# The output stage's loads of merged rows, post-norm vector, kept tiles and x rows spread over products and pinned to their traced place

## The chip, the cores and the metric

One core of one Trainium2 chip. The core has a matrix engine (TensorE, PE), a vector engine (VectorE, DVE), a scalar engine (ScalarE, ACT), GpSimd (POOL) and a sync engine (SyncE, SP); in this kernel nearly every DMA is issued from SP's queue. The metric is device microseconds of the whole program; the time before is the median of three runs.

## The reference

One layer of a bidirectional encoder with 1024 rows and model width 2048, in float32. What the output stage computes is the last two lines of `hybrid_layer`:

```python
h = rmsnorm(x, pre_g) * (1.0 + scale[:, None]) + shift[:, None]
proj = h @ w_in
...
merged = g_a * (y_a @ w_br_attn) + g_p * (y_p @ w_br_pool)
o = merged @ w_out                                   # (1024, 2048) @ (2048, 2048)
return x + gate[:, None] * rmsnorm(o, post_g)
```

`rmsnorm` takes the mean square over all 2048 columns of a row of `o`, so a row of the output can be finished only when all of its columns are there.

## The kernel before

**Products.** Every large matrix product is made with float32 operands that are split into a high and a low part (`split`, L95 on ACT for the high part, L96 on DVE for the low part), and three matmuls: high by high, low by high, high by low. Two-by-two blocks of a product are formed with seven block products instead of eight, so sums of blocks (S1 to S4 of the weights, T1 to T4 of the moving rows) take the place of one product. S1 to S4 of `w_out` were written to DRAM (`ws_d`) earlier in the program.

**The output stage** is four calls of `out_pair(half, i, ...)`: half 0 and 1 are the first and second 512 rows, i is the first or second block of 512 columns in each half of the columns. In words below they are pairs 00, 01, 10 and 11. Each pair runs seven products in this order: A11 by B11 (bank X), S3 by T3 (V), S2 by T2 (Z), A12 by B21 (X), A22 by T4 (V), S1 by T1 (Z), S4 by B22 (Z). They are numbered n = 0 to 6 where the code says `n`. One product takes four weight loads of 512 KB, `wr`, from `ws_d` (L1174) or `w_out` (L1177), into a ring of four buffers; each load is split into two pairs `whi`, `wlo` (rings of four); 48 matmuls follow (L1183 to L1185), 24 for each of two banks, twelve for each load. A load can go when the splits of the load four before it, which had its buffer, have been made. The four loads of the next pair's A11 are issued in the middle of S4 (`first_raws`).

**Work between the products.** After each quarter of a product (jp = 0 to 3) a hook runs: `between_00` to `between_11`, by pair. In `between_00` it splits the merged rows for the next product (`put_op`, tiles `m` into `mh` on ACT and `ml` on DVE) and loads merged rows of the second half into the `m` tiles (`fetch_next`, `fetch_merged`, L1168; 16 loads of 256 KB in eight calls of two). There are eight such tiles, each filled by two loads. They hold the first half's merged rows, and a tile is free once its last split was made: the four of `kh` = 0 in the quarters of A22, the four of `kh` = 1 in those of S1. In pair 01 the sums and splits for the second half are made; in pairs 10 and 11 the first half's rows are finished (`first_rows`: a kept tile of `o` from `o_d`, L1342, and the row of x, L1209, into a ring of eight row tiles `mo`; `finish_block`, L1204, and its store, L1205), and x rows for the last rows are loaded (`xr`).

**Results.** Behind a product its banks are taken out by ACT or DVE (`p7`, `u2`, `c11`, `u4`), squared with a row sum on ACT (`square`, L1193), and multiplied with the post-norm vector `pg` (`result`, L1273; `pg` is loaded by `fetch_gain`, L1229, in two loads). Pair 00 stores its results to `o_d` (L1277); the other pairs keep them.

**Order.** A scheduler sets the order of each engine's instructions, by its own estimates, except for instructions given to `keep`: such an instruction keeps its place behind the one traced before it on its engine. All loads and stores of the stage (`load`, `store`) are issued by SP in the order of its program. An issue that waits for its buffer, or for its data, holds all that are behind it.

Of the kernel before, what the change touches and what calls it, by code (L numbers as in the profile page):

```python
# [12 lines left out]
F32 = mybir.dt.float32  # L13
# [7 lines left out]
P = 128  # L21
# [21 lines left out]
def encoder_layer(ctx: ExitStack, tc: tile.TileContext, x, c, table, w_ada, b_ada, pre_g,  # L43
# [16 lines left out]
    x = x[0]  # L60
# [4 lines left out]
    def pool(name, bufs=1, **kw):  # L65
        return tc.tile_pool(name=name, bufs=bufs, reuse_waits="tile", **kw)
# [9 lines left out]
    def uid(s):  # L76
        cnt[0] += 1
        return f"{s}_{cnt[0]}"
# [4 lines left out]
    def slot(name, dt=F32R, shape=(P, 512)):  # L83
        return big.tile(list(shape), dt, tag="big", name=uid(name))
# [5 lines left out]
    def keep(ins):  # L90

        tc.keep_in_program_order(ins)
# [14 lines left out]
    load = nc.sync.dma_start  # L107
# [15 lines left out]
    JP = KT // 4  # L123
# [9 lines left out]
    o_d = dram.tile([S // 2, D], F32, name="o_d")  # L133
    ws_d = {n: dram.tile([D // 2, D // 2], F32, name=f"ws_d{n}") for n in ("S1", "S2", "S3", "S4")}
    m_d = dram.tile([D, S], F32, name="m_d")
    pg_d = dram.tile([1, D], F32, name="pg_d")
# [215 lines left out]
    for r0, src in ((0, c[0]), (16, b_ada[0, 0:D]), (32, b_ada[0, D:2 * D]),  # L352
                    (48, pre_g[0]), (64, b_merge[0]), (96, pool_scale[0])):
        n = src.shape[0] // P
# [421 lines left out]
    held = {}  # L776
# [38 lines left out]
    with pool("attn") as ap:  # L815
# [27 lines left out]
        qraw, q, bt, g, pr, pv, opened = {}, {}, {}, {}, {}, {}, []  # L843
# [240 lines left out]
    for b, w in enumerate((w_ba, w_bp)):  # L1084
# [4 lines left out]
        else:  # L1089
# [4 lines left out]
            mr = ctx.enter_context(pool("mraw", side="right"))  # L1094

            def merged_tiles():

                return [[mr.tile([P, 2, 512], F32, tag="m", name=uid("m"), bufs=2 * JP) for _ in range(JP)]
                        for _ in range(2)]
# [65 lines left out]
    def fetch_merged(m, kh, jp):  # L1165
        for n in range(2):
            k = 2 * (2 * jp + n) + kh
            load(m[kh][jp][:, n], m_d[k * P:(k + 1) * P, 512:1024])  # L1168

    def weights(name, i, jp):  # L1170

        raw = wp.tile([P, 2, 512], F32, tag="raw", name=uid("wr"), bufs=4)
        if name in ws_d:
            load(raw, ws_rows(name)[:, 2 * jp:2 * jp + 2, i * 512:(i + 1) * 512])  # L1174
        else:
            n0 = (name[1] == "2") * (D // 2) + i * 512
            load(raw, wo_rows(int(name[2]) - 1)[:, 2 * jp:2 * jp + 2, n0:n0 + 512])  # L1177
        return raw

    def out_mm(pb, op, name, j, t, w, first, last):  # L1180
        ts_ = slice(t * P, (t + 1) * P)
        hi, lo = (o_[:, j % 2, ts_] for o_ in op[name][j // 2])
        nc.tensor.matmul(pb, hi, w[0], start=first, stop=False, skip_group_check=True)  # L1183
        nc.tensor.matmul(pb, lo, w[0], start=False, stop=False, skip_group_check=True)  # L1184
        nc.tensor.matmul(pb, hi, w[1], start=False, stop=last, skip_group_check=True)  # L1185

    xrow, held = {}, {}
# [18 lines left out]

    def fetch_x_block(T, n, tile_of):
        xrow[T, n] = tile_of("xr")
        load(xrow[T, n], x[T * P:(T + 1) * P, n * 512:(n + 1) * 512])  # L1209

    def row_tiles():
        m = mr.tile([P, 2, 512], F32, tag="m", name=uid("mo"), bufs=2 * JP)
# [4 lines left out]
    def out_pair(half, i, op, between, after=None):  # L1217
# [5 lines left out]
        g = {}  # L1223

        def fetch_gain():
            for nh in range(2):
                g[nh] = ev.tile([P, 512], F32, tag="ev", name=uid("pg"))
                n0 = nh * (D // 2) + i * 512
                load(g[nh], pg_d[0:1, n0:n0 + 512].to_broadcast([P, 512]))  # L1229

        def split_weights(wname, ring=True, pin=()):
            for jp in range(JP):
                raw = first_raws.pop(0) if wname == "A11" and first_raws else weights(wname, i, jp)
                for jj in range(2):
                    hi, lo = (wp.tile([P, 512], F32R, tag=t, name=uid(t), bufs=4) if ring else slot(t)
                              for t in ("whi", "wlo"))
                    split(hi, lo, raw[:, jj], 2 * jp + jj in pin)
                    yield hi, lo


        def product(wname, mov, pbs, fresh=False):

            ws = split_weights(wname)
            n, nj = next(count), 2 * JP
            for j in range(nj - 2):
                w = next(ws)
                for t in range(2):
                    out_mm(pbs[t], op, mov, j, t, w, fresh and j == 0, False)
                if j % 2:
                    between(n, j // 2)  # L1250
            w = list(ws)
            if n == 6:
                first_raws.extend(weights("A11", 1 - i, jp) for jp in range(JP))
            for t in range(2):
                for j in (nj - 2, nj - 1):
                    out_mm(pbs[t], op, mov, j, t, w[j - nj + 2], False, j == nj - 1)
            between(n, JP - 1)
# [5 lines left out]
        def copies(ts, pbs):  # L1263
            for t in range(2):
                nc.scalar.activation(ts[t], pbs[t], AF.Copy)
            return ts
# [12 lines left out]
        def kept(tag):  # L1279

            return list(row_tiles()) if half == 1 and i == 0 else tiles(tag)
# [1 line left out]
        bx, bz, bv = ([bank(tag, b) for tag in tags] for b, tags in  # L1283
                      (("X", ("mm", "mm")), ("Z", SEEDED), ("V", ("sc", "sc"))))
        product("A11", "B11", bx, True)
        fetch_gain()
        for t in range(2):
            nc.scalar.activation(bz[t], bx[t], AF.Copy)
        product("S3", "T3", bv, True)
        p7 = copies(kept("p7"), bv)  # L1290
        product("S2", "T2", bz)
        u2 = copies(kept("u2"), bz)
# [31 lines left out]
            for n in (0, 2, 3, 1):  # L1324
                finish_block(6 + t, n, scale)

    nextm, nextt2 = [], {}
    scales = {}
    side = deque()

# [2 lines left out]
    def first_rows(T, n):  # L1333

        def place(name):
            ring.rotate(-1)
            return ring[-1]

        def fetch():
            if (T, n) not in held:  # L1340
                held[T, n] = place("fo")
                load(held[T, n], o_d[T * P:(T + 1) * P, n * 512:(n + 1) * 512])  # L1342
            fetch_x_block(T, n, place)

        def put_out():
            if T not in scales:
                scales[T] = row_scale(T)
            finish_block(T, n, scales[T])

        return fetch, put_out  # L1350
# [6 lines left out]
    later = deque((kh, jp) for kh in range(2) for jp in range(JP))  # L1357

    def fetch_next():
        if later:  # L1360
            fetch_merged(nextm, *later.popleft())

    def between_00(n, jp):
        if n < 6:
            put_op(n + 1, jp, ops[0], mt, mt2)
        if n == 4 and jp == JP - 1:
            nextm.extend(merged_tiles())
        if n >= 5 and jp:
            fetch_next()

    def between_01(n, jp):

        if n == 0 and jp:
            fetch_next()
        if n == 1:
            merged_sums(nextm, nextt2, jp)
        for k in ((), (), (0,), (1, 2), (3,), (4,), (5,))[n]:
            put_op(k, jp, ops[1], nextm, nextt2)
# [17 lines left out]
    def between_11(n, jp):  # L1396
        if jp % 2 and n < 3:
            steps(1)
        if jp == JP - 1 and n in (2, 4):
            for T in (4, 5) if n == 2 else (6, 7):  # L1400
                for b in range(4):
                    fetch_x_block(T, b, lambda name: slot(name, F32))

    def third_block():
        assert not side
# [47 lines left out]
```

## Time and profile before

| | us |
|---|---|
| median of three runs | 2126.83 |
| lowest and highest of them | 2126.15, 2128.21 |
| the profiled execution's own time | 2129.34 |
| its span | 2127.5 |
| output stage: first matmul of A11 of pair 00 | 1804.94 |
| first matmul of A11 of pairs 01, 10, 11 | 1886.33, 1964.17, 2040.47 |
| last matmul ends | 2119.05 |

The granted clock of PE is 0.999 in the profiled execution, so it takes no part in what follows. PE, DVE, ACT and POOL are the engines; SP's queue of issues is shown as SPq. A row of a timeline has the start of an instruction from the span's start in us, its duration, engine, source line, operation, output and inputs by the program's names (numbers left out), and in brackets the idle time before it on its engine, with the instruction that ended it. "A <- B" in a list of waits says that A's engine was idle until B, with the total in us, how often, and the longest. For a DMA issue the duration is the time until the queue went on, with all waits for its condition in it; "to landing" is from the issue to the arrival of the data. Product starts are times of the first matmul of a product on PE.

### The profile page before, as it was taken

The numbers are of one execution on the slowest core, as the hardware profiler recorded it, in microseconds if no ns is written. First come the engines' busy times: TensorE is split into PE (matmuls) and PEld (weight loads), VectorE is DVE, ScalarE is ACT, GpSimd is POOL, SyncE is SP. The second block draws the span as 40 slices with busy tenths as digits, with TensorE's granted clock in tenths as the row PEclk, the third lists the DMA queues.
The fourth block names the chain that finished last, engine by engine and source line by source line (L and its number), as shares of the span: only waits on it lengthen the run. The fifth ranks groups of instructions, "written<-read, shape, count | busy, mean of one in ns | idle before, by whom it ended". The sixth has DMA issues, their size and how long they took to land.

```text
span 2127.5 us, 28921 instructions
## 1 busy us (share of the span) xinstructions
PE 2091.2 (98%) x9567; PEld 1713.4 (81%) x9567; DVE 1536.2 (72%) x2754; ACT 1106.6 (52%) x2102; POOL 7.4 (0%) x66
## 2 busy tenths in 40 slices
PE   6999999999999999999999999999999999999998
PEld 3588888887888888888888888888788788878876
DVE  5786667777547776677777678856857977879667
ACT  5654444444474544665656444333645644768655
POOL 0000000000000000000000000000000000000000
PEclk9999999999999999999999999999999999999999
DMA  9886566899676355544645576765745654686896
GB/s 327 272 269 217 186 206 224 301 309 315 223 232 207 122 177 200 169 162 159 201 145 164 158 243 221 224 210 187 252 158 174 218 184 161 225 294 220 303 303 244
DMA packets 303255, 466.10 MB, mean 219 GB/s; under 512 B 23883, under 2 KB 144867, under 8 KB 303105
## 3 DMA queue, kind: packets, MB, share of 16 engines
q1 hardware_dynamic: 301648, 462.02, 66.0%
q0 software_dynamic: 1120, 2.19, 0.3%
q8 instruction: 75, 1.23, 0.2%
q14 instruction: 76, 0.61, 0.1%
q10 hardware_dynamic: 336, 0.06, 0.0%
HBM read 340.41 MB, written 125.85 MB: 219 GB/s over the span
## 4 chain that ended last, share of the span: by engine, by line
PE 88%; DVE 5%; DMA 4%; issue 1%; ACT 1%; SPq 1%; ACTq 0%; DVEq 0%
PE Z L235 30%; PE X L235 20%; PE V L235 20%; PE Z L1183 2%; PE Z L1184 2%; PE Z L1185 2%; PE V L1185 1%; PE V L1183 1%; PE V L1184 1%; DMA raw<-in_w_merge_dram 1%; PE GEMV L455 1%; PE X L1185 1%; DVE wlo L96 1%; PE X L1184 1%; PE X L1183 1%; PE PT L905 1%
## 5 line engine op out<-in xcount | busy, mean ns | idle before, releaser
L95 ACT ACTIVATE whi<-raw 128x512 fp32r<-128x512 f32 (+1 forms) x528 | 321.3, 610 | 509.7 <-PE Z L235 254.3
L96 DVE TENSOR_TENSOR wlo<-raw,whi 128x512 fp32r<-128x512 f32 (+1 forms) x528 | 347.4, 662 | 183.7 <-PE Z L235 132.8
L96 DVE TENSOR_TENSOR wlo<-wr,whi 128x512 fp32r<-128x512 f32 x224 | 151.1, 689 | 60.9 <-ACT whi L95 58.4
L95 ACT ACTIVATE whi<-wr 128x512 fp32r<-128x512 f32 x224 | 138.7, 629 | 93.5 <-DVE wlo L96 37.2
L102 DVE TENSOR_TENSOR raw<-raw,raw 128x512 f32<-128x512 f32 x80 | 55.2, 690 | 107.0 <-DMA raw<-in_w_merge_dram 79.1
L235 PE MATMUL V<-T3h,whi 128*128 128x512 f32 x336 | 92.1, 393 | 0.7 <-DVE u L102 0.5
L235 PE MATMUL Z<-T2h,whi 128*128 128x512 f32 x336 | 91.6, 392 | 0.8 <-ACT whi L95 0.7
L235 PE MATMUL X<-B11h,whi 128*128 128x512 f32 x336 | 92.1, 392 | 0.0
L235 PE MATMUL Z<-B22h,whi 128*128 128x512 f32 x336 | 91.6, 392 | 0.5 <-ACT u L290 0.5
L235 PE MATMUL V<-T4l,whi 128*128 128x512 f32 x336 | 91.2, 390 | 0.7 <-DVE T4l L96 0.6
L235 PE MATMUL V<-T4h,whi 128*128 128x512 f32 x336 | 91.4, 391 | 0.2 <-ACT T4h L95 0.2
L235 PE MATMUL Z<-T1h,whi 128*128 128x512 f32 x336 | 91.6, 390 | 0.0
L235 PE MATMUL X<-B11l,whi 128*128 128x512 f32 x336 | 91.0, 390 | 0.0
L235 PE MATMUL X<-B21h,whi 128*128 128x512 f32 x336 | 91.0, 391 | 0.0
L235 PE MATMUL Z<-T2h,wlo 128*128 128x512 f32 x336 | 90.8, 390 | 0.1
L235 PE MATMUL X<-B21l,whi 128*128 128x512 f32 x336 | 90.8, 390 | 0.0
L235 PE MATMUL Z<-B22l,whi 128*128 128x512 f32 x336 | 90.7, 390 | 0.0
L235 PE MATMUL Z<-T1l,whi 128*128 128x512 f32 x336 | 90.7, 389 | 0.0
L235 PE MATMUL X<-B11h,wlo 128*128 128x512 f32 x336 | 90.7, 390 | 0.0
L235 PE MATMUL Z<-B22h,wlo 128*128 128x512 f32 x336 | 90.6, 390 | 0.1
L235 PE MATMUL V<-T3l,whi 128*128 128x512 f32 x336 | 90.6, 389 | 0.0
L235 PE MATMUL Z<-T1h,wlo 128*128 128x512 f32 x336 | 90.6, 389 | 0.0
(308 smaller groups left out, 4771.7 us busy)
## 6 DMA issues: line engine op xcount, KB each, us to landing
part<-part_d SPq DMA_DIRECT2D x136, 256.0 KB, 4.9
ada<-in_w_ada_dram SPq DMA_DIRECT2D x128, 256.0 KB, 5.4
raw<-in_w_in_dram SPq DMA_DIRECT2D x64, 512.0 KB, 4.0
raw<-in_w_merge_dram SPq DMA_DIRECT2D x64, 512.0 KB, 5.8
wr<-ws_dS SPq DMA_DIRECT2D x64, 512.0 KB, 5.6
wr<-in_w_out_dram SPq DMA_DIRECT2D x48, 512.0 KB, 5.1
proj_d<-part SPq DMA_DIRECT2D x68, 256.0 KB, 2.3
sw<-in_w_out_dram SPq DMA_DIRECT2D x64, 256.0 KB, 5.5
```

The lines of the kernel that those rows point to most:

```text
L95: ins = (nc.scalar.activation(hi, src, AF.Copy), nc.vector.tensor_tensor(lo, src, f32(hi), ALU.subtract))
L96: nc.vector.tensor_tensor(lo, src, f32(hi), ALU.subtract))
L102: return (eng or nc.vector).tensor_tensor(o, a, b, ALU.add)
L235: nc.tensor.matmul(ps, w_[:, i], op[mov][j][m_], start=fresh and i == 0 and n == 0, stop=i == nj - 1 and n == 2, skip_group_check=True)
L455: ins = nc.tensor.matmul(pv[g:g + 32, :], scz[:, kc, :], tile_of(kc), start=kc < 4, stop=kc >= 12, tile_position=(0, g))
L905: nc.tensor.transpose(pt[:, i * P:(i + 1) * P], p[:, i * P:(i + 1) * P], ident)
L1183: nc.tensor.matmul(pb, hi, w[0], start=first, stop=False, skip_group_check=True)
L1184: nc.tensor.matmul(pb, lo, w[0], start=False, stop=False, skip_group_check=True)
L1185: nc.tensor.matmul(pb, hi, w[1], start=False, stop=last, skip_group_check=True)
```

## The change

No operation is added or removed. Seven edits:

1. The loads of `fetch_merged` (`m`) are given to `keep`.
2. The loads of x rows (`fetch_x_block`) are given to `keep`.
3. The loads of `pg` are given to `keep`, and `fetch_gain` is called behind S3 instead of behind A11.
4. The reloads of kept tiles from `o_d` in `first_rows` are given to `keep`.
5. The tiles for the second half's merged rows are taken one by one as each is fetched, not all eight at the end of A22.
6. The eight calls of `fetch_next` move: before, one each at the last three quarters of S1 and of S4, and two more at A11 of pair 01 (`jp` 1 to 3, of which the first two have work left); now one each at the last three quarters of A22, the last three of S1, and the first two of S4 (`n == 6` calls it in every quarter; the list is empty after the second).
7. The 16 `xr` loads of pair 11 move: before, eight at the end of S2 and eight at the end of A22; now the four column blocks of one row tile over each of S2, A12, A22 and S1, one load a quarter.

```diff
--- before.py
+++ after.py
@@ -1165,7 +1165,7 @@
     def fetch_merged(m, kh, jp):
         for n in range(2):
             k = 2 * (2 * jp + n) + kh
-            load(m[kh][jp][:, n], m_d[k * P:(k + 1) * P, 512:1024])
+            keep(load(m[kh][jp][:, n], m_d[k * P:(k + 1) * P, 512:1024]))
 
     def weights(name, i, jp):
 
@@ -1206,7 +1206,7 @@
 
     def fetch_x_block(T, n, tile_of):
         xrow[T, n] = tile_of("xr")
-        load(xrow[T, n], x[T * P:(T + 1) * P, n * 512:(n + 1) * 512])
+        keep(load(xrow[T, n], x[T * P:(T + 1) * P, n * 512:(n + 1) * 512]))
 
     def row_tiles():
         m = mr.tile([P, 2, 512], F32, tag="m", name=uid("mo"), bufs=2 * JP)
@@ -1226,7 +1226,7 @@
             for nh in range(2):
                 g[nh] = ev.tile([P, 512], F32, tag="ev", name=uid("pg"))
                 n0 = nh * (D // 2) + i * 512
-                load(g[nh], pg_d[0:1, n0:n0 + 512].to_broadcast([P, 512]))
+                keep(load(g[nh], pg_d[0:1, n0:n0 + 512].to_broadcast([P, 512])))
 
         def split_weights(wname, ring=True, pin=()):
             for jp in range(JP):
@@ -1283,10 +1283,10 @@
         bx, bz, bv = ([bank(tag, b) for tag in tags] for b, tags in
                       (("X", ("mm", "mm")), ("Z", SEEDED), ("V", ("sc", "sc"))))
         product("A11", "B11", bx, True)
-        fetch_gain()
         for t in range(2):
             nc.scalar.activation(bz[t], bx[t], AF.Copy)
         product("S3", "T3", bv, True)
+        fetch_gain()
         p7 = copies(kept("p7"), bv)
         product("S2", "T2", bz)
         u2 = copies(kept("u2"), bz)
@@ -1324,7 +1324,7 @@
             for n in (0, 2, 3, 1):
                 finish_block(6 + t, n, scale)
 
-    nextm, nextt2 = [], {}
+    nextm, nextt2 = [[], []], {}
     scales = {}
     side = deque()
 
@@ -1339,7 +1339,7 @@
         def fetch():
             if (T, n) not in held:
                 held[T, n] = place("fo")
-                load(held[T, n], o_d[T * P:(T + 1) * P, n * 512:(n + 1) * 512])
+                keep(load(held[T, n], o_d[T * P:(T + 1) * P, n * 512:(n + 1) * 512]))
             fetch_x_block(T, n, place)
 
         def put_out():
@@ -1358,20 +1358,18 @@
 
     def fetch_next():
         if later:
-            fetch_merged(nextm, *later.popleft())
+            kh, jp = later.popleft()
+            nextm[kh].append(mr.tile([P, 2, 512], F32, tag="m", name=uid("m"), bufs=2 * JP))
+            fetch_merged(nextm, kh, jp)
 
     def between_00(n, jp):
         if n < 6:
             put_op(n + 1, jp, ops[0], mt, mt2)
-        if n == 4 and jp == JP - 1:
-            nextm.extend(merged_tiles())
-        if n >= 5 and jp:
+        if n in (4, 5) and jp or n == 6:
             fetch_next()
 
     def between_01(n, jp):
 
-        if n == 0 and jp:
-            fetch_next()
         if n == 1:
             merged_sums(nextm, nextt2, jp)
         for k in ((), (), (0,), (1, 2), (3,), (4,), (5,))[n]:
@@ -1396,10 +1394,8 @@
     def between_11(n, jp):
         if jp % 2 and n < 3:
             steps(1)
-        if jp == JP - 1 and n in (2, 4):
-            for T in (4, 5) if n == 2 else (6, 7):
-                for b in range(4):
-                    fetch_x_block(T, b, lambda name: slot(name, F32))
+        if 2 <= n < 6:
+            fetch_x_block(2 + n, jp, lambda name: slot(name, F32))
 
     def third_block():
         assert not side
```

What this does to the order is shown at three places. Rows have the line, the kind, the output and the input with the program's numbers, and the tile's shape; "x2" stands for two equal rows.

The first is SP in pair 00, from the first load of S1's weights, over products A22, S1 and the start of S4 (`wr<-ws_dS1` and `wr<-ws_dS4` are weights of S1 and S4, `m<-m_d` merged rows, `o_d<-c11` and `o_d<-u2` results that go out). Before:

```order
L1174 DMA wr_3610_17563<-ws_dS1_95 128x2x512
L1168 DMA m_3600_17545<-m_d_99 128x512
L1277 DMA o_d_94<-c11_3568_17431 128x512
L1174 DMA wr_3617_17589<-ws_dS1_95 128x2x512
L1277 DMA o_d_94<-c11_3569_17432 128x512
L1168 DMA m_3600_17545<-m_d_99 128x512
L1174 DMA wr_3624_17617<-ws_dS1_95 128x2x512
L1168 DMA m_3601_17546<-m_d_99 128x512 x2
L1174 DMA wr_3631_17645<-ws_dS1_95 128x2x512
L1168 DMA m_3602_17547<-m_d_99 128x512 x2
L1174 DMA wr_3642_17687<-ws_dS4_98 128x2x512
L1277 DMA o_d_94<-u2_3538_17323 128x512
```

With the change:

```order
L1168 DMA m_3586_17493<-m_d_99 128x512
L1277 DMA o_d_94<-c11_3568_17431 128x512
L1168 DMA m_3586_17493<-m_d_99 128x512
L1277 DMA o_d_94<-c11_3569_17432 128x512
L1168 DMA m_3594_17522<-m_d_99 128x512 x2
L1168 DMA m_3602_17551<-m_d_99 128x512 x2
L1174 DMA wr_3612_17590<-ws_dS1_95 128x2x512
L1168 DMA m_3619_17616<-m_d_99 128x512 x2
L1174 DMA wr_3620_17619<-ws_dS1_95 128x2x512
L1168 DMA m_3627_17645<-m_d_99 128x512 x2
L1277 DMA o_d_94<-u2_3538_17323 128x512
L1174 DMA wr_3628_17648<-ws_dS1_95 128x2x512
```

The second to fourth loads of S1 (`wr_3617`, `wr_3624`, `wr_3631` before) had at most two `m` loads of one tile between them and stood ahead of the store of the first `u2`; now (`wr_3612`, `wr_3620`, `wr_3628`) six `m` loads stand ahead of the second, two more ahead of each of the others, and the fourth follows that store.

At the same time, on ACT, where S4's weights are split and S1's bank is taken out (`u4`), `p7` squared. Before:

```order
L95 ACTIVATE whi_3643_17689<-wr_3642_17687 128x512
L95 ACTIVATE whi_3645_17699<-wr_3642_17687 128x512
L1265 ACTIVATE u4_3638_17673<-Z_3446_16993 128x512
L95 ACTIVATE whi_3648_17711<-wr_3647_17709 128x512
L95 ACTIVATE whi_3650_17721<-wr_3647_17709 128x512
L1265 ACTIVATE u4_3639_17674<-Z_3447_16994 128x512
L1193 ACTIVATE junk_3640_17678,ssq_o_14114<-p7_3508_17211 128x512
L95 ACTIVATE whi_3653_17735<-wr_3652_17733 128x512
```

With the change:

```order
L1265 ACTIVATE u4_3636_17677<-Z_3446_16993 128x512
L95 ACTIVATE whi_3641_17693<-wr_3640_17691 128x512
L95 ACTIVATE whi_3643_17703<-wr_3640_17691 128x512
L1265 ACTIVATE u4_3637_17678<-Z_3447_16994 128x512
L1193 ACTIVATE junk_3638_17682,ssq_o_14114<-p7_3508_17211 128x512
L1193 ACTIVATE junk_3639_17687,ssq_o_14114<-p7_3509_17212 128x512
L95 ACTIVATE whi_3647_17718<-wr_3646_17716 128x512
L95 ACTIVATE whi_3649_17728<-wr_3646_17716 128x512
```

The first copy of `u4` now stands ahead of the first split of S4, and both squares of `p7` ahead of the third.

The second place is SP from the last stores of pair 00 to the weights of S3 of pair 01 (`o_d<-u4` are the results of S4). Before:

```order
L1277 DMA o_d_94<-u4_3666_17789 128x512
L1168 DMA m_3607_17552<-m_d_99 128x512
L1277 DMA o_d_94<-u4_3667_17790 128x512
L1168 DMA m_3607_17552<-m_d_99 128x512
L1229 DMA pg_3692_17889<-pg_d_100 128x512
L1229 DMA pg_3693_17891<-pg_d_100 128x512
L1174 DMA wr_3694_17895<-ws_dS3_97 128x2x512
L1174 DMA wr_3700_17920<-ws_dS3_97 128x2x512
```

With the change:

```order
L1277 DMA o_d_94<-u4_3666_17793 128x512
L1174 DMA wr_3692_17891<-ws_dS3_97 128x2x512
L1277 DMA o_d_94<-u4_3667_17794 128x512
L1174 DMA wr_3698_17916<-ws_dS3_97 128x2x512
L1174 DMA wr_3704_17941<-ws_dS3_97 128x2x512
L1174 DMA wr_3710_17966<-ws_dS3_97 128x2x512
L1229 DMA pg_3716_17991<-pg_d_100 128x512
L1229 DMA pg_3717_17993<-pg_d_100 128x512
```

The `m` and `pg` loads are gone from between the stores and S3's weights; the `pg` loads stand behind all four weights.

The third place is SP from the second half of S4 of pair 10 to S3 of pair 11 (`wr<-in_w_out` are A11's weights, `mo<-o_d` reloads and `mo<-in_x` x rows into a row tile, `out<-mo` stores of finished rows). Before:

```order
L1177 DMA wr_4061_19312<-in_w_out_dram 128x2x512
L1342 DMA mo_3920_18695<-o_d_94 128x512
L1177 DMA wr_4062_19314<-in_w_out_dram 128x2x512
L1205 DMA out_0_dram<-mo_3921_18696 128x512
L1209 DMA mo_3920_18695<-in_x_dram 128x512
L1209 DMA mo_3921_18696<-in_x_dram 128x512
L1174 DMA wr_4090_19439<-ws_dS3_97 128x2x512
L1342 DMA mo_3921_18696<-o_d_94 128x512
L1205 DMA out_0_dram<-mo_3918_18693 128x512
L1174 DMA wr_4095_19461<-ws_dS3_97 128x2x512
L1174 DMA wr_4100_19485<-ws_dS3_97 128x2x512
L1174 DMA wr_4105_19507<-ws_dS3_97 128x2x512
```

With the change:

```order
L1177 DMA wr_4061_19312<-in_w_out_dram 128x2x512
L1177 DMA wr_4062_19314<-in_w_out_dram 128x2x512
L1342 DMA mo_3919_18694<-o_d_94 128x512
L1209 DMA mo_3919_18694<-in_x_dram 128x512
L1205 DMA out_0_dram<-mo_3921_18696 128x512
L1342 DMA mo_3920_18695<-o_d_94 128x512
L1209 DMA mo_3920_18695<-in_x_dram 128x512
L1174 DMA wr_4088_19435<-ws_dS3_97 128x2x512
L1205 DMA out_0_dram<-mo_3918_18693 128x512
L1342 DMA mo_3921_18696<-o_d_94 128x512
L1209 DMA mo_3921_18696<-in_x_dram 128x512
L1174 DMA wr_4093_19457<-ws_dS3_97 128x2x512
```

Two more of A11's weights stand ahead of the reload into `mo_3920`, and its x row and that of `mo_3919` directly behind their reloads; S3's first weight stands behind the reload into `mo_3920` and its second behind that into `mo_3921`, as before.

## The prediction

> **What bounds the kernel now.** I read the page's engine table first, then the list of waits cut to the output stage, then the timeline of PE, then that of SP's queue.
>
> ```profile
> span 2127.5 us, 28921 instructions
> PE 2091.2 (98%) x9567; PEld 1713.4 (81%) x9567; DVE 1536.2 (72%) x2754; ACT 1106.6 (52%) x2102; POOL 7.4 (0%) x66
> ```
>
> PE is idle for 36 of 2127.5 us in the whole program, so an edit that only moves loads can win no more than the part of that which loads cause. The waits of PE from 1785 us on (us in total, times, longest):
>
> ```profile
> PE V L1183 <- ACT whi L95: 2.4, 2, 1.4
> PE X L1185 <- DVE wlo L96: 1.2, 1, 1.2
> PE Z L235 <- ACT u L290: 0.5, 1, 0.5
> ```
>
> Only the first row can be a load: a split waits for its weights. The two others lie where the branch stage runs out, before any moved load. The idle column is less than the loss, since the matmuls behind a late split also come late, so I take product starts. The timeline of PE, at the first matmuls of ten products:
>
> ```profile
> 1864.41 0.39 PE L1183 MATMUL Z<-whi,mh 128*128 128x512 f32 x1
> 1875.29 0.39 PE L1183 MATMUL Z<-whi,mh 128*128 128x512 f32 x1
> 1886.33 0.39 PE L1183 MATMUL X<-whi,mh 128*128 128x512 f32 x1
> 1898.34 0.50 PE L1183 MATMUL V<-whi,mh 128*128 128x512 f32 x1 [0.97 <-ACT whi L95]
> 1909.63 0.39 PE L1183 MATMUL Z<-whi,mh 128*128 128x512 f32 x1
> 2040.47 0.39 PE L1183 MATMUL X<-whi,mh 128*128 128x512 f32 x1
> 2051.35 0.39 PE L1183 MATMUL V<-whi,mh 128*128 128x512 f32 x1
> 2064.24 0.39 PE L1183 MATMUL Z<-whi,mh 128*128 128x512 f32 x1
> 2075.11 0.39 PE L1183 MATMUL X<-whi,mh 128*128 128x512 f32 x1
> 2086.21 0.39 PE L1183 MATMUL V<-whi,mh 128*128 128x512 f32 x1
> ```
>
> A product without a stall lasts 10.88 us (2040.47 to 2051.35: 48 matmuls, so 1.36 us for each of its eight k tiles, and 2.72 for one weight load of two). A11 and S3 of pair 01 take 23.30 instead of 21.76: 1.54 lost. S3 of pair 11 takes 12.89: 2.01 lost. Its A12 takes 11.10: 0.22 lost. Together 3.77 us, all that loads cost PE here.
>
> Why those are late stands in SP's timeline (SP issues in order, and an issue whose condition is not met holds all behind it):
>
> ```profile
> 1888.41 0.32 SPq L1277 DMA_DIRECT2D o_d<-u  x1
> 1888.77 0.43 SPq L1168 DMA_DIRECT2D m<-m_d  x1
> 1889.25 0.94 SPq L1229 DMA_DIRECT2D pg<-pg_d  x2
> 1890.28 9.72 SPq L1174 DMA_DIRECT2D wr<-ws_dS  x5
> ...
> 2046.77 0.33 SPq L1342 DMA_DIRECT2D mo<-o_d  x1
> 2047.66 1.55 SPq L1174 DMA_DIRECT2D wr<-ws_dS  x3
> ...
> SPq L1342 <- DMA out_dram<-mo: 14.7, 4, 5.0
> ```
>
> At 1890.28 the first weights of S3 stand behind two stores, m rows and both pg loads. At 2047.66 the second of pair 11's S3 stands behind a reload of a row tile that waits for that tile's store to land: SP stood still for 14.7 us in four such waits.
>
> **The change, part by part.** It adds and removes no operation: 16 m loads, 8 pg, 16 x rows into row tiles, 16 xr, 8 reloads, as before. It changes who stands behind whom.
>
> *What it takes away.* At pair 01's start no m and no pg is ahead of S3 any more. Its first load follows the first of the two o_d stores, so it goes out before 1888.41 rather than at 1890.28, and its split, due at 1886.33+10.88 = 1897.21, has some 9 us. I count the whole 1.54. At pair 11's start all four A11 loads now precede the reload that waits, and S3's first two loads lose one such wait ahead of them. The second, needed two k tiles after 2051.35 (2054.07), then depends on the store behind a split near 2043 rather than on 2047.66: about 3 us earlier, against 1.40 to 2.01 of stall. I count 2.01, and 0.22 for A12, whose loads no longer wait behind eight x rows. Bounds: 1.5 (only pair 01's) to 3.77; taken 3.77.
>
> *What it moves into the way.* In pair 00 the merged rows come one product earlier and ahead of weights. Before, S1's second to fourth loads went out as soon as their buffers were free, and a store of u2 came after them:
>
> ```profile
> 1855.01 0.37 SPq L1174 DMA_DIRECT2D wr<-ws_dS  x1
> 1857.61 0.37 SPq L1174 DMA_DIRECT2D wr<-ws_dS  x1
> 1860.33 0.37 SPq L1174 DMA_DIRECT2D wr<-ws_dS  x1
> 1866.29 0.32 SPq L1277 DMA_DIRECT2D o_d<-u  x1
> ```
>
> Now each stands behind m loads that wait until the last split of the tile they overwrite, and the fourth also behind that store. The DVE and ACT work that they wait for, and the time to landing of four 512 KB weight loads issued at 1860.33, 1866.89, 1871.21 and 1876.68, then of all of them in the stage:
>
> ```profile
> 1857.50 0.69 DVE L96 TENSOR_TENSOR ml<-m,mh 128x512 fp32r<-128x512 f32 x1
> 1865.58 0.68 DVE L1273 TENSOR_TENSOR u<-u,pg 128x512 f32<-128x512 f32 x1
> 1878.52 0.69 DVE L1273 TENSOR_TENSOR p<-p,pg 128x512 f32<-128x512 f32 x1
> ...
> 1874.13 0.60 ACT L1265 ACTIVATE u<-Z 128x512 f32<-128x512 f32 x1 [0.95 <-PE Z L1185]
> 1874.62 1.27 ACT L95 ACTIVATE whi<-wr 128x512 fp32r<-128x512 f32 x2
> ...
> DMA to landing us min/median/max: 5.8/5.8/5.8
> DMA to landing us min/median/max: 5.2/5.2/5.2
> DMA to landing us min/median/max: 7.0/7.0/7.0
> DMA to landing us min/median/max: 4.1/4.1/4.1
> ...
> DMA to landing us min/median/max: 3.7/5.4/9.5
> ```
>
> S1, second load: the split of 1857.50 ends at 1858.19, two m issues of 0.43 follow, so it goes at 1859.1 (was 1855.01), lands at 1864.9 (5.8). Its splits (0.64 by ACT, 0.69 by DVE) end at 1866.3; due at 1864.41+2.72 = 1867.13. No stall, but u2's add and product queue behind them on DVE (0.6 and 0.68) and end at 1867.6 rather than 1866.26.
> S1, fourth load: behind that store, so at 1868.0 (was 1860.33); landing 5.2 later, 1873.2; split by 1873.85; due at 1864.41+6x1.36 = 1872.57. Stall 1.3, and 0.2 more because DVE's half ends 0.69 behind ACT's where the matmuls leave 0.45: **1.5**. With 3.7 to landing nothing queues and it is 0; with 6.1 (m's median) 2.8.
> S4, first loads: ACT now copies u4 out of the bank before it splits them. From 1874.13 the copy, two splits, the second copy and two squares (0.6 to 0.77 each) put the third split at 1878.5, due at 1875.29+2.72 = 1878.01; with DVE's order alike I take **0.7** (0.3 to 1.0).
> S4, fourth load: behind both p7 stores, whose product ended at 1878.52+0.69 = 1879.2, now 1.5 later; issued near 1881.1, landed (5.4, between the 7.0 and 4.1 beside it) at 1886.5, split by 1887.1; due at 1875.29+1.5+0.7+8.16 = 1885.65. Stall 1.5, and 0.2 as above: **1.7** (0.2 to 2.5).
> S4's third load, by the same steps, comes just in time: 0.
>
> By the Trainium skill (DMA: Bandwidth & Descriptors, "Latency and other measured facts") a DMA's fixed cost falls when memory is less loaded. The row of 4.1 agrees with it and that of 7.0, both next to m loads or without them, leaves it open; by the rule the sum would be the second rival's.
>
> *What costs nothing.* pg is first used when A12 ends, three products on; xr not before 2105, in the tail, and its last load now goes near 2093; if that cover failed, a load would be one landing late, 5.4. The end itself:
>
> ```profile
> 2118.66 0.39 PE L1185 MATMUL Z<-wlo,mh 128*128 128x512 f32 x1
> 2120.02 0.68 DVE L1273 TENSOR_TENSOR c<-Z,pg 128x512 f32<-128x512 f32 x1
> ```
>
> The last product is taken 0.97 us after PE's last matmul ends, behind ACT's square; no load stands there.
>
> **Sum.** Losses 1.5+0.7+1.7 = 3.9 (0.5 to 6.3), gains 3.77 (1.5 to 3.77): +0.1 us, on the profiled execution's 2129.3 (its span is 2127.5). The median of the three runs, 2126.83, is 2.5 below that execution; the same difference on it gives **2126.9**. Its own range, with landings of 4.6 to 6.1 for the moved loads: 2125.4 to 2129.2.
>
> **Rivals.**
> *The stalls stay away* (ends faster). Weight loads that go out later meet an emptier queue: between 1864 and 1869 nothing but one store would be issued. With landings of 3.7 to 4.1 the losses are 0.5 to 1.0: 2126.83-3 = 2123.8, at best 2123.3. For it: 4.1 at 1876.68. Against it: what is issued between 1852 and 1873 is nearly the same bytes as before, and the DMA share of that stretch is full:
>
> ```profile
> 1855.00:1865.00 10.00, 10.00 (x46) 8.29 (x45) 8.28 (x14) 6.81 (x14) 0.00 (x0) 1.00 1.01 362
> ```
>
> (the last two numbers are that share and GB/s.)
> *A convoy in pair 00* (ends slower). The m loads wait for splits of S1, S1's loads wait behind m, and the splits wait for S1's loads: a circle with no slack once a landing exceeds 6.1. From there each further us comes twice on the fourth load of S1 (through the store and in its own landing) and again on S4. At 7.0 throughout: S1's stall 4.6, S4's 0.7 and 3.4, sum 8.7: +4.9, 2131.8; at 6.1 it is +2.5, 2129.3. For it: the 7.0 and the full queue. Against it: a late PE also delays what it needs next.
> The skill's rule that a DMA is issued early and waited for late (DMA: Bandwidth & Descriptors, "Rules for kernel authors") speaks against putting S1's loads back, and so for this rival.
> *The change doesn't do what it says* at pair 11: the row tiles' reloads still wait for stores in front of S3, as before, and only 1.54 is won: 2126.83+3.9-1.5 = 2129.2. Against it: two more A11 loads and one S3 load are ahead of those waits.
>
> **How the numbers follow.** Forecast 0.47, stalls away 0.25, convoy 0.20, no help at pair 11 0.08. 0.2% is 4.25 us, about what a measurement of this kernel can tell from no change. Faster than that needs more than all 3.77 us: 0.03. Slower needs the convoy above 6.8 us to landing: 0.09. Else no change: 0.88. The range reaches from the best of the second case to the lower half of the convoy: 2123.2 to 2130.6.
>
> **What would show it.** Right: V of pair 01 starts 10.88 after its X; S3 of pair 11 lasts 10.9; in pair 00 PE waits for splits in the last quarter of S1 (near 1872.6) and of S4 (near 1885), 1 to 2 us each; SP's S1 loads go at about 1859, 1862 and 1868. Wrong: no such waits in pair 00 (then 2123 to 2124), waits already in S1's second quarter (the convoy), or a wait left in V at 2054.

## The result

The changed kernel takes 2131.45 us (median of 16 runs, 2127.48 to 2137.79); the kernel before took 2126.36 in 16 runs (2124.51 to 2129.91). The ratio is 1.0018 with a 95% interval of 1.0011 to 1.0025: 3.8 us slower, 2.3 to 5.3 (the quotient of the two medians would be 1.0024; the interval belongs to the ratio). In a second timing beside the kernel before it was 1.0021 (1.0011 to 1.0032). So the change costs a little under 0.2%, where the forecast was 2126.9 and no change. The median lies 0.85 above the range of the prediction; the first ratio on the median known then, 2126.83 x 1.0018, gives 2130.7, its upper end.

The page of the changed kernel, span and engine table. PE is as busy as before (2091.2 there), and its span is 3.2 us longer, so the loss is idle time of PE:

```profile
span 2130.7 us, 28916 instructions
PE 2091.0 (98%) x9567; PEld 1714.1 (80%) x9567; DVE 1538.2 (72%) x2754; ACT 1106.7 (52%) x2102; POOL 7.5 (0%) x66
```

The list of PE's waits in the output stage of the changed kernel (total, times, longest). The row on V is the one that stood there before with 2.4 in two waits; the rows on Z are new:

```profile
PE Z L1183 <- ACT whi L95: 3.8, 3, 1.9
PE V L1183 <- ACT whi L95: 1.4, 1, 1.4
PE X L1185 <- DVE wlo L96: 1.2, 1, 1.2
PE Z L1183 <- ACT u L1265: 0.4, 1, 0.4
```

The timeline of PE in the changed kernel: the matmuls that waited in S1 and S4 of pair 00 and in S3 of pair 11, and the starts of products around them.

```profile
1863.17 0.39 PE L1183 MATMUL Z<-whi,mh 128*128 128x512 f32 x1
1873.37 0.50 PE L1183 MATMUL Z<-whi,mh 128*128 128x512 f32 x1 [1.86 <-ACT whi L95]
1877.16 0.50 PE L1183 MATMUL Z<-whi,mh 128*128 128x512 f32 x1 [0.47 <-ACT whi L95]
1887.61 0.50 PE L1183 MATMUL Z<-whi,mh 128*128 128x512 f32 x1 [1.51 <-ACT whi L95]
1890.47 0.39 PE L1183 MATMUL X<-whi,mh 128*128 128x512 f32 x1
1912.23 0.39 PE L1183 MATMUL Z<-whi,mh 128*128 128x512 f32 x1
2053.96 0.39 PE L1183 MATMUL V<-whi,mh 128*128 128x512 f32 x1
2058.22 0.50 PE L1183 MATMUL V<-whi,mh 128*128 128x512 f32 x1 [1.38 <-ACT whi L95]
2066.78 0.39 PE L1183 MATMUL Z<-whi,mh 128*128 128x512 f32 x1
```

S1 and S4 of pair 00 take 1890.47 - 1863.17 = 27.30 us instead of 21.92. A11 and S3 of pair 01 take 1912.23 - 1890.47 = 21.76, which is two products without a stall, instead of 23.30. S3 of pair 11 still takes 12.82 (12.89 before): its wait did not go.

Why S1's and S4's weights are late stands in SP's timeline of the changed kernel. Behind it is the row of ACT that PE waited for at 1877.16, the split of S4's first load:

```profile
1857.84 0.40 SPq L1174 DMA_DIRECT2D wr<-ws_dS  x1
1859.69 0.80 SPq L1168 DMA_DIRECT2D m<-m_d  x2
1860.53 0.43 SPq L1174 DMA_DIRECT2D wr<-ws_dS  x1
1862.41 1.07 SPq L1168 DMA_DIRECT2D m<-m_d  x2
1866.44 0.32 SPq L1277 DMA_DIRECT2D o_d<-u  x1
1866.81 0.44 SPq L1174 DMA_DIRECT2D wr<-ws_dS  x1
1867.65 0.32 SPq L1277 DMA_DIRECT2D o_d<-u  x1
1868.29 0.86 SPq L1168 DMA_DIRECT2D m<-m_d  x2
1869.20 0.50 SPq L1174 DMA_DIRECT2D wr<-ws_dS  x1
...
1879.66 1.20 SPq L1277 DMA_DIRECT2D o_d<-p  x2
1880.91 0.43 SPq L1174 DMA_DIRECT2D wr<-ws_dS  x1
```

```profile
1876.47 1.15 ACT L95 ACTIVATE whi<-wr 128x512 fp32r<-128x512 f32 x2 [0.54 <-DMA wr<-ws_dS]
```

The fourth load of S1 goes out at 1866.81, behind m loads and the store of u2: 3.64 us after S1's start, where before it went 4.08 ahead of it (1860.33 against 1864.41; 1863.0 there is already S4's first). S4's first load goes at 1869.20, 6.0 after S1's start, behind the second store of u2 and two m loads; ACT waits 0.54 for it to land. S4's fourth goes at 1880.91, behind both stores of p7. The three largest of SP's own waits in this part of the changed kernel, from 1850 to 1892, are these conditions:

```profile
SPq L1168 <- DVE ml L96: 7.0, 8, 2.6
SPq L1277 <- DVE u L1273: 5.1, 3, 2.9
SPq L1277 <- DVE p L1273: 3.5, 2, 3.0
```

The time to landing of the loads issued at 1866.81, 1871.14 (S4's second) and 1880.91, in the changed kernel:

```profile
DMA to landing us min/median/max: 5.8/5.8/5.8
DMA to landing us min/median/max: 7.9/7.9/7.9
DMA to landing us min/median/max: 5.9/5.9/5.9
```

And what moved from 1864 to 1882, first row the changed kernel, second row the kernel before:

```profile
DMA packets 3211, 6.00 MB, mean 333 GB/s; under 512 B 283, under 2 KB 283, under 8 KB 3211
```

```profile
DMA packets 3197, 6.02 MB, mean 334 GB/s; under 512 B 260, under 2 KB 260, under 8 KB 3197
```

The bytes there are nearly the same. What changed is the order in which they were asked for.

### The profile page after: what moved, and what is told of

It is laid out like the page before. It is cut to its first block, busy times and chain, and to the rows that moved or that the text cites. A ratio compares the mean times of both kernels' runs of the same rounds, so it can differ in the third digit from the quotient of the medians.

```text
span 2130.7 us, 28916 instructions
## 1 busy us (share of the span) xinstructions
PE 2091.0 (98%) x9567; PEld 1714.1 (80%) x9567; DVE 1538.2 (72%) x2754; ACT 1106.7 (52%) x2102; POOL 7.5 (0%) x66
## 4 chain that ended last, share of the span: by engine, by line
PE 86%; DVE 6%; DMA 5%; ACT 1%; issue 1%; SPq 0%; ACTq 0%; DVEq 0%; POOL 0%; POOLq 0%
PE Z L235 29%; PE X L235 19%; PE V L235 19%; PE Z L1183 1%; PE Z L1184 1%; PE Z L1185 1%; DMA wr<-ws_dS 1%; PE V L1185 1%; PE V L1183 1%; PE V L1184 1%; PE X L1185 1%; PE X L1184 1%; PE X L1183 1%; DVE wlo L96 1%; DMA xt<-in_x_dram 1%
```

## The experiments

One profile shows one execution. So the runs were read by product, from the first matmul of one to that of the next on PE. Two products without a stall take 21.76 us, a whole pair 76.16. The last S1 and S4 reach only to the start of the last matmul, so pair 11 without a stall would be 75.93. "Stage" is from the first matmul of S3 of pair 00 to that. What lies ahead has the same order on every engine in every kernel, but for pair 00's two pg loads, which edit 3 puts behind two m_d stores and three of S3's weight loads (its end varies from 1819.6 to 1824.2). "End" is from the start of the last matmul to the end of the span, which the page gives to 0.1. In us:

| kernel | S1+S4, 00 | A11+S3, 01 | pair 11 | S3 of 11 | stage | end | ratio of times |
|---|---|---|---|---|---|---|---|
| before | 21.92 | 23.30 | 78.19 | 12.89 | 297.77 | 8.84 | |
| before again | 21.91 | 23.64 | 77.82 | 10.88 | 297.74 | 8.75 | |
| the change | 27.30 | 21.76 | 78.60 | 12.82 | 302.03 | 9.02 | 1.0018 |
| again | 27.17 | 21.76 | 77.29 | 12.18 | 300.58 | 8.94 | |
| third | 29.51 | 21.76 | 77.32 | 12.27 | 302.96 | 9.09 | 1.0021 |
| merged-row edits alone | 28.10 | 22.00 | 76.02 | 10.88 | 300.52 | 9.25 | 1.0020 |
| all but those | 21.93 | 21.76 | 78.43 | 12.79 | 296.49 | 9.20 | 1.0002 |
| again | 21.91 | 22.24 | 76.13 | 10.87 | 294.66 | 9.11 | 0.9995 |
| fetches two quarters later | 29.48 | 21.78 | 75.98 | 10.88 | 301.65 | 9.27 | 1.0032 |
| fetches in S1 and S4 | 23.35 | 21.76 | 76.56 | 10.98 | 296.04 | 9.23 | 1.0010 |
| rows spread evenly | 21.90 | 21.86 | 75.93 | 10.88 | 294.07 | 9.61 | 0.9997 |
| again | 21.91 | 22.01 | 76.10 | 10.88 | 294.40 | 9.87 | 0.9999 |

**All but the merged-row edits.** The change with edits 1, 5 and 6 taken back:

```diff
-            keep(load(m[kh][jp][:, n], m_d[k * P:(k + 1) * P, 512:1024]))
+            load(m[kh][jp][:, n], m_d[k * P:(k + 1) * P, 512:1024])
...
-        if n in (4, 5) and jp or n == 6:
+        if n == 4 and jp == JP - 1:
+            nextm.extend(merged_tiles())
+        if n >= 5 and jp:
             fetch_next()
...
+        if n == 0 and jp:
+            fetch_next()
```

> The change without its merged-row edits: m loads at the calls of before and not kept; pg, x rows, kept tiles as in the change. Theory (the m loads' place in SP's queue costs pair 00 its time, pg in front of S3 cost pair 01): S1 plus S4 of pair 00 take 21.9 us as before (27.3 with the change); A11 plus S3 of pair 01 take 21.8 to 22.3 (23.30 before); S3 of pair 11 stays at 12.8. The time is 1 to 2 us under before. Rival (the kept loads themselves cost it): S1 plus S4 stay above 24 and the time is 2 or more above before.

Measured: 21.93 in pair 00, 21.76 at the start of pair 01, 12.79 for S3 of pair 11, ratio 1.0002 (0.9993 to 1.0011). The loss in pair 00 belongs to the merged-row edits, and the other edits alone win the start of pair 01. The time did not fall by the 1 to 2 us expected. Its profile lost 0.5 in front of the last S4, which the table's pair 11 holds. The 12.8 expected for S3 of pair 11 came by luck: the second profile of this kernel has 10.87.

**The merged-row edits alone**, in the kernel before (edits 1, 5, 6):

> Before with the merged-row edits alone. Theory: S1 plus S4 of pair 00 take 26.5 to 28 us (21.92 before); A11 plus S3 of pair 01 about 22.3, since pg is still ahead of S3 but m is not; pair 11 as before, S3 12.9. The time is 4 to 5 us above before. Rival (it takes all edits together): S1 plus S4 under 24, time within 2 of before.

Measured: 28.10 in pair 00, 22.00 at the start of pair 01, ratio 1.0020 (1.0011 to 1.0030): as the theory has it, to 0.1 in pair 00 and 0.3 in pair 01. But S3 of pair 11 took 10.88, though the order of SP's queue is the same there as before. The theory had 12.9, so this was a first sign that this stall is not set by the order.

In the change built without the keep on the m loads alone, the order of SP's queue comes out row for row the same. So it is the earlier calls that put the loads there, not the pin.

**Fetches two quarters later:**

```diff
-        if n in (4, 5) and jp or n == 6:
+        if n == 4 and jp > 2 or n == 5 or n == 6 and jp < 3:
             fetch_next()
```

> The change with its eight fetches two quarters later: the fourth weight load of S1 then stands ahead of the store of u2, the fourth of S4 still behind both stores of p7. Theory (a late issue behind waiting m loads and stores): S1 of pair 00 takes at most 11.3 us, S4 still loses 1 to 2.5 in its last quarter, together 22.8 to 24.3 (27.3 with the change). Rival (the m bytes in these products slow the landings, whatever the order): nearly the same bytes move in the same products, so together 26 to 27.5.

Measured: 29.48, the ratio 1.0032 (1.0020 to 1.0044). Both theories missed. The matmuls of S1 lost nothing, as the theory of the queue says and its rival, the theory of bytes, does not: its fourth load now goes ahead of the store of u2. But S4's first matmul came 1.4 us late (12.28 after S1's, where at most 11.3 was expected), and S4 lost another 6.2: together 7.6. PE's timeline of this kernel:

```profile
1876.88 0.50 PE L1183 MATMUL Z<-whi,mh 128*128 128x512 f32 x1 [1.24 <-ACT u L1265]
1879.04 0.50 PE L1183 MATMUL Z<-whi,mh 128*128 128x512 f32 x1 [0.51 <-ACT u L1265]
1889.69 0.79 PE L1183 MATMUL Z<-whi,mh 128*128 128x512 f32 x1 [3.55 <-ACT whi L95]
```

The first two wait for a copy of S1's bank (u4) by ACT. In ACT's order that copy stands behind the splits of S4's first load, which was issued at 1868.53 and landed 6.6 us later. So a late load holds PE twice: its own matmuls, and the bank that ACT has not emptied. The third is S4's fourth load:

```profile
1879.26 0.32 SPq L1277 DMA_DIRECT2D o_d<-p  x1
1879.68 0.87 SPq L1168 DMA_DIRECT2D m<-m_d  x2
1881.67 0.32 SPq L1277 DMA_DIRECT2D o_d<-p  x1
1882.04 0.43 SPq L1174 DMA_DIRECT2D wr<-ws_dS  x1
```

It stands behind both stores of p7, which come late because p7 needs the delayed copies of u4, and lands 6.9 us later. The circle of the convoy is here: a late load delays a result, whose store delays the next load.

**Fetches at all quarters of S1 and S4:**

```diff
-        if n in (4, 5) and jp or n == 6:
+        if n > 4:
             fetch_next()
```

> The change with its eight fetches at all quarters of S1 and S4, three to four quarters later: no weight load of S1 stands behind a store of u2, none of S4 behind the stores of p7, and one pair of m loads is left between S4 and pair 01. Theory: S1 plus S4 of pair 00 21.8 to 22.5 us, A11 plus S3 of pair 01 21.8 to 22.3, time 1 to 2 us under before. Rival (bytes): 25 to 27, time 2 or more above before.

Measured: 23.35 and 21.76, ratio 1.0010 (1.0001 to 1.0019). Nearer to the queue theory's 21.8 to 22.5 than to the 25 to 27 of bytes, yet missed by 0.85, and the time did not fall by 1 to 2 us. What is left is one wait, in PE's and then ACT's timeline of this kernel:

```profile
1878.52 0.50 PE L1183 MATMUL Z<-whi,mh 128*128 128x512 f32 x1 [1.30 <-ACT u L1265]
```

```profile
1874.77 0.60 ACT L1265 ACTIVATE u<-Z 128x512 f32<-128x512 f32 x1 [0.63 <-PE Z L1185]
1876.84 1.15 ACT L95 ACTIVATE whi<-wr 128x512 fp32r<-128x512 f32 x2 [1.47 <-DMA wr<-ws_dS]
1877.89 0.58 ACT L1265 ACTIVATE u<-Z 128x512 f32<-128x512 f32 x1
```

ACT waits 1.47 us for S4's second load between the two copies of u4, and PE waits for the second copy. The same wait appears in the last S4 of some profiles (the 0.4 on u in the list of the changed kernel above).

**Two profiles more.** The kernel before, and the change, unaltered:

> The kernel before, profiled once more. Theory (what the order in SP's queue sets comes back in every execution, what saturated DMA sets does not): S1 plus S4 of pair 00 21.9 us and A11 plus S3 of pair 01 22.8 to 23.6 again; S3 of pair 11, 12.89 in the first profile, may be anything from 10.9 to 13, since kernels with the same order there gave 10.88. Rival (the order sets pair 11 too): 12.7 to 13.0 again.

> The changed kernel, profiled once more. Theory: S1 plus S4 of pair 00 26 to 29 us and A11 plus S3 of pair 01 21.8 again; S3 of pair 11 anything from 10.9 to 13 (12.82 first), the last S1 plus S4 21.5 to 22.3 (22.25 first). Rival (the order sets pair 11 too): 12.7 to 12.9 again, and 22.2 for the last.

Measured: S1 and S4 of pair 00 21.91 and 27.17, the start of pair 01 23.64 and 21.76: these come back. S3 of pair 11 takes 10.88 in the kernel before and 12.18 in the change, with pair 11 as a whole at 77.82 and 77.29. In the second profile of the kernel before its losses sit in S2, A12 and the last S4 instead. So the place and size of pair 11's stall differ from one execution of the same kernel to the next, and the rival falls: the order alone does not set them.

**Rows spread evenly.** All but the merged-row edits, and two of the steps that finish rows moved out of S4 of pair 10 and A11 of pair 11; xr over three products instead of four:

```diff
-        elif jp % 2:
+        elif jp % 2 and (n < 6 or jp == 1):
             steps(1)
...
-        if jp % 2 and n < 3:
+        if jp % 2 and n < 3 and (n or jp == 1):
             steps(1)
-        if 2 <= n < 6:
-            fetch_x_block(2 + n, jp, lambda name: slot(name, F32))
...
+    xs = deque((T, b) for T in range(4, 8) for b in range(4))
...
+        for _ in range(2 if jp == JP - 1 or n == 5 and jp == 1 else 1):
+            if n > 2:
+                fetch_x_block(*xs.popleft(), lambda name: slot(name, F32))
```

> The change without its merged-row edits, with the finished rows of the first half spread more evenly: one step instead of two in S4 of pair 10 and in A11 of pair 11, all 16 xr loads over A12, A22 and S1 of pair 11. S3's first two weights of pair 11 then stand ahead of every reload that waits. Theory (full DMA and waiting reloads around 2045 make S3's second load late): S3 of pair 11 10.9 to 11.1, its weights land within 7 us, no new stall; 1.5 to 2.5 us under before. Rival (the bytes come back elsewhere): S2 to S1 of pair 11 lose as much, time within 1 of before.

Measured: no stall in pair 11, S3 10.88, stage 294.07. The landing of the weight loads issued while A11 of pair 11 runs: the change, then this kernel:

```profile
DMA to landing us min/median/max: 6.3/8.7/9.0
```

```profile
DMA to landing us min/median/max: 5.6/5.8/6.4
```

PE's waits in the output stage of this kernel:

```profile
PE X L1185 <- DVE wlo L96: 1.2, 1, 1.2
PE Z L235 <- ACT u L290: 0.6, 1, 0.6
PE X L1183 <- DVE u L102: 0.4, 1, 0.4
```

The engines are near full in both: their share in the two halves of A11 of pair 11 is 0.98 and 0.92 in the change, 0.92 and 0.95 here, and this kernel even moves a little more in that stretch (3.24 MB, 3.10 in the change). What it does is to put S3's first two loads ahead of the reloads that wait: the second goes out 9.4 us ahead of S3's start, not 5.2, and lands 6.0 later, not 8.6. These are the rows of SP's queue with that load, each with the load's time to landing; in the change it is the first of the row's two, here the second, at 2043.84:

```profile
2048.80 0.90 SPq L1174 DMA_DIRECT2D wr<-ws_dS  x2
DMA to landing us min/median/max: 8.6/8.6/8.6
```

```profile
2041.00 3.22 SPq L1174 DMA_DIRECT2D wr<-ws_dS  x2
DMA to landing us min/median/max: 6.0/6.0/6.0
```

The earlier issue alone would have been enough: with 8.6 the load would still be there 0.8 before S3 starts. Why the landing is shorter too was not tried apart.

Over all twelve profiles the landing of this second load, counted from S3's start, tells the stall: 2.8 to 3.5 us behind it in the five with S3 at 12.18 to 12.89, at most 1.6 behind it in the seven with 10.87 to 10.98. Both its parts vary: in the two profiles of the kernel before it goes out 3.7 and 4.7 ahead of S3 and takes 7.2 and 5.8 to land. SP's order in pair 11 is that of before in three profiles (the merged-row edits alone is the third), of which one has the stall, and that of the change in seven, of which four have it, all three of the change itself among them. So neither order has the stall in every execution; whether the new one has it more often can't be told from so few.

In the list of PE's waits above no weight load is left, and all three lie at the border to the branch stage. But the ratio is 0.9997 (0.9986 to 1.0008), which is the rival's "within 1 of before" and not the 1.5 to 2.5 expected, though no stall came back elsewhere on PE. Where a part of the 3.7 us went shows at the end of this kernel:

```profile
2118.29 0.39 PE L1185 MATMUL Z<-wlo,mh 128*128 128x512 f32 x1
```

```profile
2120.43 0.68 DVE L1273 TENSOR_TENSOR c<-Z,pg 128x512 f32<-128x512 f32 x1
```

The last product is taken 2.14 us after the start of PE's last matmul, not 1.36 as before (2118.66 and 2120.02). DVE is behind with the finished rows, and 0.8 of the gain is waited for there. In the kernel before, too, DVE comes to it, at 2120.02, from a finished row without a pause:

```profile
2119.36 0.74 DVE L1204 SCALAR_TENSOR_TENSOR c<-c,st,xr 128x512 f32<-128x512 f32 x1
```

**Timed again**, these three beside the kernel before on one chip:

> The kernel with evenly spread rows, timed again beside the two others. Its stage from S3 of pair 00 to PE's last matmul took 294.1 us (before 297.8 and 297.7, the change 302.0 and 300.6). Theory (the stage sets the time, what lies ahead of it is the same code): 294 to 295 us in the stage again, and 2 to 3.5 us under before in the time, since the end behind the last matmul was 0.8 longer. Rival (the gain is lost elsewhere, as the first timing of 0.9997 suggests): within 1 us of before.

> The changed kernel, timed again on the same chip. Theory: 300.5 to 302.5 us from S3 of pair 00 to the last matmul, 3 to 5 us above before. Rival (the first timing of 1.0018 was the chip's): within 2 us of before.

> The change without its merged-row edits, timed again. Theory: S1 plus S4 of pair 00 21.9 us, A11 plus S3 of pair 01 21.8; pair 11 loses 0 to 2.5 by chance; 295 to 297.5 us from S3 of pair 00 to the last matmul; 0 to 2.5 us under before, between before and the evenly spread kernel. Rival: no difference to before, since the mean loss in pair 11 grew by what pair 01 won.

Measured: 0.9999 (0.9990 to 1.0008), 1.0021 (1.0011 to 1.0032) and 0.9995 (0.9986 to 1.0003), with stages of 294.40, 302.96 (0.5 above what was expected) and 294.66 (0.3 under). The change's loss is confirmed. For the other two the stage is shorter by 1.3 to 3.7 us in all four profiles, and no timing tells them from the kernel before. The even spread's 3.5 us in the stage less 0.9 at the end would be 0.9988, inside the first of its intervals and just under the second. The table leaves out A11 of pair 00. It takes 15.9 us in both profiles of the kernel before and 16.7 and 17.2 in those of the even spread; with that, some 1.6 us are left of the gain, a ratio of 0.9992, which lies inside both intervals. Over all profiles A11 takes 14.5 to 16.0 in the three with pair 00's pg loads in their old place, 15.3 to 17.2 in the nine others. But the difference is there about 0.5 us before the first row of any engine's order that differs (pg, at 1807.32 before), so no edit is known to make it. It may be chance, and this part stays open. No kernel here beats the one before by what can be measured.

## Why the prediction was right or wrong

The three profiles of the change against the two before it (means, by the table): pair 00 costs 27.99 - 21.92 = 6.1, pair 01 wins 23.47 - 21.76 = 1.7, pair 11 wins 78.00 - 77.74 = 0.3, the end costs 0.2: +4.3, and the timings say 3.8 and 4.5 (0.0018 of 2126 and 0.0021 of 2130). The forecast was +0.1. Of the 4.2 between, pair 00 makes 2.2 and pair 11 makes 1.9.

*Pair 01, 1.54 won.* Right, 1.5 to 1.9. The m loads alone moved away leave 22.00, the pg loads alone 21.76 and 22.24, so either does nearly all of it: the stall was what the two of them together added ahead of S3's first load.

*Pair 11, 2.01 and 0.22 won.* Wrong, and this is the step that failed in kind. I took the stall of one profile as fixed by the order, and the wait in front of the second load as its cause. The load did go out earlier, 5.2 us ahead of S3 instead of 3.7, but not by the 3 us forecast: SP still waited 1.3 for a finished row to store and 1.7 for a store to land (3.3 before) in front of it. It then landed 8.6 us later instead of 7.2, at 2057.4, just ahead of the split that V waited for: 3.5 after S3's start in both. The stall is set by when that load lands, and this differs between two executions of the kernel before (3.5 and 1.1) by more than the new order had won. In the second profile of the kernel before, the 1.9 us that pair 11 loses lie elsewhere. A lead of 9.4 us, in the kernel with evenly spread rows, left no stall in either profile. The rival "no help at pair 11" named the right size, and its wait is there; but that wait stands in profiles without a stall too (2.6 in the second of the kernel before), so it is not the whole cause.

*S1's fourth load, 1.5.* The mechanism was right: issued 3.64 after S1's start, 3.6 by the prediction (1868.0 - 1864.41). It landed 5.8 later and not 5.2, and the stall was 2.4 (1.86 idle, and some 0.5 behind it while DVE catches up); in the other two profiles it landed 4.5 and 4.3 later, and the stall was 1.0.

*S4's first loads, 0.7.* The wrong cause. Not ACT's order of copies and splits made it, but a late first load: behind the second store of u2 and two m loads, a place whose cost the prediction did not work out. ACT waited 0.54, 1.58 and 1.26 us in the three profiles for it to land; it cost 1.2 here, 2.3 and 2.0 in the other two. The two kernels with moved fetches show the sharper form, in which PE waits for the bank that ACT copies behind a late split.

*S4's fourth load, 1.7.* Right in place: behind both p7 stores at 1880.91 (1881.1 predicted), landing 5.9 for 5.4; about 2 in two profiles, near 4.7 in the third (landing 7.1).

Together the losses are 5.4, 5.3 and 7.6 for the 3.9 predicted, with 6.3 as the bound. The terms that were mis-sized are S4's first and fourth loads; S1's fourth has the right mean. The landings under them spread wider than the forecast's own range of 4.6 to 6.1: from 4.3 (S1's fourth) to 8.0 (S4's second) in the three profiles.

The "convoy" rival priced 6.1 and 7.0 us to landing at 2.5 and 4.9 over before, and the change is 3.8 to 4.5 over it. That this fits is in part luck, since the rival counted all of the 3.77 as won; in pair 00 alone it gave losses of 6.3 and 8.7. Its sign, waits already in S1's second quarter, was not seen: the first wait is in S1's last. So the losses came where the forecast put them, but for S4's first load, at the size of its upper bound and, once, near the middle of the convoy's. The range went up to 2130.6 only because it reached into the convoy; the forecast's own ended at 2129.2.

*The stalls stay away*, because later loads meet an emptier queue: seen for S1's fourth load alone, in two of three profiles (4.5 and 4.3 to landing; 5.8 in the first profile, 5.9 and 6.9 at its old place before). S4's second took 7.5 to 8.0, where it had taken 5.2 and 5.7. Between 1864 and 1882 the DMA moved 333 GB/s where it had moved 334. On the Trainium skill's rule (DMA: Bandwidth & Descriptors, "Latency and other measured facts") that lighter load shortens a DMA's fixed cost this run says nothing, since the load was not lighter. The Trainium skill's rule to issue early and wait late (DMA: Bandwidth & Descriptors, "Rules for kernel authors") agrees with S1's fourth load: issued 7.7 us later against its product, 2.4 us lost. The other early loads, the m loads, show its limit: an early issue whose buffer is not free holds every later one on its engine.

*What costs nothing.* pg and xr: none of PE's waits in any profile leads to them. *The end*: not ACT's square but DVE's finished rows stand in front of the last product, before and after (the square's row sum ended at 2119.83, DVE's last row led on to 2120.02). The prediction had no load there, but in front of the last S4 the copy of u4 behind a late split costs 0.4 to 0.9 in some profiles of both kernels.

## What to carry to other kernels

A load that reuses a buffer should go into an in-order queue only when the buffer is already free, and weights of the next product should be ahead of it and of every store of results. Where the DMA engines are near full, compute the stall from a range of landings seen in that stretch at full load, not from one row's, and issue the load ahead by more than the longest of them (here 9.4 us of lead left no stall, 3.7 to 5.7 left one in five profiles of ten); and before winning back a stall of a microsecond or two, profile the same kernel a second time, to see whether the stall belongs to the order or to the execution.

When PE has no stall left, look at who finishes the program: here DVE's backlog of row work took back 0.8 us of what PE won.

## What was not expected of the hardware

The time to landing of one kind of load, 512 KB of S weights, had no single value: 5.6 to 6.4 us in A11 of pair 11 with the rows spread evenly, 6.3 to 9.0 in the change, with the DMA engines near full in both (shares of 0.92 to 0.98). Two executions of one kernel differed by 1.4 us in it for the same load (7.2 and 5.8), and with 1.1 us in the time of issue this decided between a stall of 2 us and none. The same kernel's stall in pair 11 moved between products from execution to execution (12.89 and 10.88 us for S3, 10.87 and 11.34 for S2), while the products of pair 10 together took 76.30 to 76.32 in all twelve profiles.
